# One result buffer for two attentions, table rows on GpSimd's queue, the last norm's weights inside w_up's pages, and ties for late rows

## The chip, the cores and the metric

One core of a Trainium2 chip runs the whole layer in one launch. The metric is the time of the program on the device in microseconds (us), lower is better. Before the change the median of 3 runs is 2635.41 us (2632.22 to 2638.98).

## What is computed

One layer of an encoder, in float32, for 2048 tokens of 1024 features:

```
h  = RMSNorm(x) * norm_mix
z  = h @ W_in          -> q_a k_a v_a q_b k_b v_b gate_a gate_b    (1024 x 4352)
yA = attention in a window of +-128 tokens, 8 heads on 2 kv heads, ALiBi slopes, a sink logit per head
yB = attention of 8 heads on a 32 x 64 grid, 8 x 16 neighbours, a learned bias table rpb per head
x  = x + (sigmoid(gate_a)*(yA @ Wp_A) + sigmoid(gate_b)*(yB @ Wp_B)) @ W_out
x  = x + relu(RMSNorm(x)*norm_mlp @ W_up)^2 @ W_down                (1024 x 4096, 4096 x 1024)
out = RMSNorm(x) * norm_final
```

## The kernel before

**Products.** Each float32 operand is split into a high and a low part (`split`, L281: a cast on ScalarE, L282, and a subtraction on VectorE, L283), and each product of tiles is three matmuls (hi*hi, hi*lo, lo*hi: `mm3s`, L286 to L288; for narrower tiles `mm3`, L202 to L204). The large products go in seven block products instead of eight (Strassen), so that VectorE also adds and subtracts blocks ahead of the split (L279) and adds results as they leave PSUM (L279 again, and L1560 where a gate is multiplied in). TensorE is fed without a break only if these casts, subtractions and loads are early enough.

**Order.** The program is written stage by stage with generators; a scheduler with a model of times decides the order in each engine's queue, `tc.issue_after(x)` keeps what is inside it behind instruction x, and buffers (pools, rings) decide what must wait for whom. Each engine works its queue in order. Nearly all transfers are issued by SyncE (SP), in order too: a transfer that waits for its buffer holds up every transfer behind it. ScalarE issues a few, and GpSimd some (L690, L721).

**Stages, with the times at which they run in the trace.**

- *Input*, to 554 us. x is loaded in tiles of 128 tokens, normalised and transposed. `rstd_of` (L220) makes the sum of squares of a tile in two ScalarE instructions (L225) with their accumulators, an addition on VectorE (L228) and a power on GpSimd (L230); `normalised` (L233) scales on VectorE (L239) for the first four tiles and on ScalarE (L237) for the others. z is then made in column groups q = 0 to 10 (`in_quad`, `in_seeded`), each of seven products. In `in_seeded` products 1, 5 and 6 leave PSUM by a ScalarE copy to another bank or buffer (the *seeds*, L532, L535), and the next products wait for these. Between the steps of a group stands preparation: in groups 3 and 4 the normalised rows of x (L784) and their transposition (`turned_out`), and from group 9 on W_out's operands (`wo_parts`, with L687 and L688). Results go out through a ring `ze` to tables in HBM.
- *Attention A*, 554 to about 820 us, 32 units of `attn_a` (L829): scores (L844, L845), max, exp, transposes to PSUM (L863), the casts of the probabilities `ph` on ScalarE (L867) and the remainders `pl` on VectorE (L868), then the products with v (L869, L870). Between these, TensorE does the gates' columns of z as filler (`gate_tiles`, L910 ff).
- *Attention B*, to about 1120 us: 32 units of `attn_b` (L1038), 4 per head: scores (L1056) of `qb` with `kb`, the bias added and the max taken (L1061), exp (L1067), scaling on GpSimd (L1072), transposes (L1084), casts `phb` (L1090) and remainders `plb` (L1091), the products with `vb` (L1096). `load_k` (L1029) loads one head's `kb` in three transfers (L1033 to L1035), L1046 loads `vb`. `make_bias_b` (L1009) loads rows of a table into `braw` (L1018, on SP), and GpSimd adds the masks (L1024). Filler is again `gate_tiles`, then `proj_tiles` (yA @ Wp_A), for which `y_pages` (L938) loads yA and splits it in eight casts (L948) and eight subtractions (L949).
- *Merge and W_out*, about 1120 to 1415 us, in two halves m of the tokens: `gated` (L1544) does yB @ Wp_B and the gates, `out_operands` (L1451) loads W_out's prepared parts from HBM into the ring `pgl` (`wo_d`, L1458; 6 places) and splits the left operands into the same ring, `out_products` (L1472) does the seven products, each in two halves of 24 matmuls, product 1's result copied between PSUM banks by L1498. In m = 1, rows of half 0 are normalised, transposed on VectorE (L249), multiplied by norm_mlp (`turned_gain`, L254) and written to HBM (`h2d`, L257).
- *w_up and w_down*, from about 1380 us to the end: `up_right` (L1299) makes the split pages of h2 for the seven products, `up_quad` (L1370) does them.

**PSUM and the change of attentions.** The four PSUM pools of the attentions are made in the order mm, s, pt, av (L800). SBUF's left side holds for A: dist, sta, qa, ka1, va1, sa, ya, ph, pl; after it, in the same addresses, for B: sb0, sb1, sb2, vb0, vb1, vb2, phb, plb, yb. So what of B lies on what of A decides how early B's loads may start. `ya` has two buffers of 64 partitions, `yb` one of B's own.

Of the kernel before, what the change touches and what calls it, by code (L numbers as in the profile page):

```python
# [92 lines left out]
def encoder_layer(ctx, tc, x, norm_mix, w_in, b_gate, sink, rpb, w_pa, w_pb, w_out,  # L93
# [126 lines left out]
    def rstd_of(pl, t, jp=None, mean=False, small=False):  # L220

        st = T(pl, [P, 4], F32, "st", 4)
        junk = T(pl if jp is None else jp, [P, 512], mybir.dt.bfloat16 if small else F32, "junk", 1)
        for n in range(2):
            A.activation(junk, t[:, n * 512 : (n + 1) * 512], AF.Square, scale=float(D) ** -0.5 if mean else 1.0,  # L225
                         accum_out=st[:, n : n + 1])
# [6 lines left out]
    def normalised(pl, tiles, jp=None, by_scalar=False, small=False):  # L233

        for t in tiles:
            if by_scalar:
                A.activation(t, t, AF.Copy, scale=rstd_of(pl, t, jp, True, small))  # L237
            else:
                V.tensor_scalar(t, t, rstd_of(pl, t, jp), float(D) ** 0.5, ALU.mult, ALU.mult)  # L239

    def turned_out(d, ht, tiles, g, gain=None):
# [9 lines left out]
        if gain is not None:  # L251
            (step, n), _ = gain.ap
            gv = bass.AP(gain.tensor, gain.offset + 8 * g, [[step, n], [1, 8], [0, P]])
            V.tensor_tensor(out=h3, in0=h3, in1=gv, op=ALU.mult)  # L254
# [4 lines left out]
    def turned_gain(t, norm):  # L259

        for a in range(4):
            SY.dma_start(t[32 * a : 32 * a + 32, 32:64], norm[0].rearrange("(j i) -> j i", i=32))
        V.transpose(out=t[:, 0:32], in_=t[:, 32:64])
        return t[:, 0:32]
# [247 lines left out]
    ORDER_3 = (1, 5, 6, 2, 7, 3, 4)  # L512

    def in_seeded(c, w, lf, right, b0=0):
# [3 lines left out]
        for n in ORDER_3:  # L518
            hl, (rh, rl) = next(lf), right[n]
            for a in range(w // P):  # L520
# [9 lines left out]
                if n == 1:  # L530
                    y[a] = zbank(ypool[a])
                    A.copy(y[a], ps)  # L532
                elif n == 5:
                    c22[a] = in_c()
                    A.copy(c22[a], ps)  # L535
                elif n == 6:
                    u2[a] = in_c()
                    A.copy(u2[a], ps)
# [15 lines left out]
    def scaled_less(out, ps, k, t):  # L554
        V.scalar_tensor_tensor(out=out, in0=ps, scalar=g_mix[:, k : k + 1], in1=t, op0=ALU.mult, op1=ALU.subtract)
# [24 lines left out]
    normalised(xp, tiles[0])  # L580
# [14 lines left out]
    normalised(xp, tiles[1], by_scalar=True)  # L595
# [112 lines left out]
    def h1_sums(k):  # L708
# [6 lines left out]
        yield  # L715
        for t, p in ((lo, 0), (hi, 1)):
            scaled(t, t, 4 * p + k)
# [38 lines left out]
    right2, n_wo = {}, [0]  # L756
    for q in range(2, len(QUADS)):
        prep, steps, b0 = iter(()), 1, 0
# [7 lines left out]
        elif q == len(QUADS) - 1:  # L766
            prep = h1_last(right2)
        elif q >= SECOND and QUADS[q][1] == 256:
            n_wo[0] += 1
            prep = wo_parts(n_wo[0], own)  # L770
# [20 lines left out]
        for _ in prep:  # L791
            pass
# [7 lines left out]
    pps.update({t: pool(f"pp_{t}", space=PSUM, stack=s_pp) for t in ("mm", "s", "pt", "av")})  # L800
    s_w = ExitStack()
    wp = pools(s_w, "right", ("raw", "whl", "z"), "w")
    s_a = ExitStack()
    ap_ = pools(s_a, "left", ("dist", "sta", "qa", "ka1", "va1", "sa", "ya", "ph", "pl"), "a")
# [12 lines left out]
    marks, began = [], []  # L817

# [10 lines left out]
    def attn_a(g, i):  # L829
# [41 lines left out]
        t = T(ap_, [64, 512], F32, "ya", 2)  # L871
        A.copy(t, po[64:128, :])
        V.tensor_tensor(out=t, in0=po[0:64, :], in1=t, op=ALU.add)
# [64 lines left out]
    def y_pages(b0):  # L938

        for b in (b0, b0 + 1):  # L940
            ypages[b] = [in_page[(6, 3, 1, 2)[b]]() for _ in range(2)]
            for g in range(2):
                SY.dma_start(halves(ypages[b][1])[g].bitcast(F32),
                             y_a[g][:, b * BT : (b + 1) * BT].rearrange("(c p) t -> p c t", p=P))
        with tc.issue_after(casts[min(now[0] + 4, len(casts) - 1)]):
            for b in (b0, b0 + 1):
                for h, l in zip(*map(halves, ypages[b])):
                    A.copy(h, l.bitcast(F32))  # L948
                    V.tensor_tensor(out=l, in0=l.bitcast(F32), in1=h.bitcast(F32), op=ALU.subtract)  # L949

# [34 lines left out]
    for n, g, m in ((4, 0, 0), (9, 0, 1), (14, 1, 1)):  # L985
        drive((attn_a(*u) for u in units_a[at:n]), live, False)
# [4 lines left out]
    drive((attn_a(g, i) for g, i in units_a[14:]), live, True)  # L991
# [11 lines left out]
    yb = T(bp, [P, BT], F32, "yb", 1)  # L1003
# [5 lines left out]
    def make_bias_b(h, jt):  # L1009
        j = (0, 1, 3)[jt]  # L1010
        w = B_W[j]
        t = T(bp, [P, 40 * w], F32, "biasl" if jt == 1 else "biass", 1 if jt == 1 else 2)
# [4 lines left out]
        with tc.issue_after(began[20]):  # L1017
            SY.dma_start(raw, src)  # L1018
# [89 lines left out]
    def all_b():  # L1108
        for h in range(BH):
            k = load_k(h)  # L1110

            for n, j in enumerate((0, 3, 1, 2) if h == 0 else range(4)):
                if j != 2:
                    bias = make_bias_b(h, JT[j])
# [20 lines left out]
    s_b.close()  # L1135
    s_pg = ExitStack()
# [36 lines left out]
    p4x = pools(s_wo, "left", ("junk", "gt", "ht", "xr"), "m")  # L1173
# [5 lines left out]
    gain = turned_gain(T(p4x, [P, P], F32, "gt", 1), norm_mlp)  # L1179
# [119 lines left out]
    def up_right(m):  # L1299
# [10 lines left out]
        def parts(n, src):  # L1310
            hi, lo = up_page[n](), up_page[n]()
            for s, h, l, e in zip(halves(src), halves(hi), halves(lo), (V, V)):
                last = split(s, h, l, e)
# [3 lines left out]
        def less(out, a, c):  # L1317
            for o, x, y in zip(halves(out), halves(a), halves(c)):
                add(V, o, x, y, ALU.subtract)
# [26 lines left out]
        less(t, b12, b11)  # L1346
        parts(1, b11)
        parts(5, t)
        yield
        b22 = block(up_rings["raw"](), 1, 1)  # L1350
        less(b12, b22, b12)
        less(t, b22, t)
# [3 lines left out]
        parts(2, b21)  # L1356
        yield right
        parts(7, b12)
        less(b21, b21, t)
        parts(4, b21)  # L1360
        parts(3, b22)
# [89 lines left out]
    def out_operands(ms):  # L1451


        def half(n, h):
# [3 lines left out]
            SY.dma_start(w.bitcast(F32), wo_d[n][h].rearrange("k p z c -> p k z c"))  # L1458
# [9 lines left out]
        for n in ORDER_O:  # L1468
            for h in range(2):
                yield half(n, h)  # L1470
# [65 lines left out]
    for m in range(2):  # L1536
# [268 lines left out]
```

## Time and profile before

| | |
|---|---|
| median of 3 runs | 2635.41 us (2632.22 to 2638.98) |
| the profiled execution | 2637.54 us |
| its span, first to last instruction | 2635.7 us |
| TensorE busy | 2555.2 us, 11936 matmuls |
| before TensorE's first matmul / after its last | 7.8 us / 8.3 us |
| VectorE, ScalarE, GpSimd busy | 1712.1, 1307.6, 342.0 us |
| DMA | 553.22 MB, 210 GB/s over the span |

The span is 1.8 us shorter than the execution's own time, and the execution is 2.1 us above the median. The table of TensorE's waits names, for each line, what released it, the sum, the count and the longest. A table of windows gives busy time by engine in a stretch, then the TensorE clock granted in it (1.00 is full, 0.50 half), the busy share of the 16 DMA engines and GB/s.

### The profile page before, as it was taken

To read this page: it belongs to the slowest core of one execution; us is meant where nothing else is said; L and a number is where in the kernel's file an instruction comes from. 1 tells how busy PE (TensorE), PEld (TensorE's weight loads), DVE (VectorE), ACT (ScalarE), POOL (GpSimd) and SP (SyncE) were. 2 spreads that over 40 slices of the span, in tenths; PEclk is the share of its full clock that TensorE was granted. 3 is DMA by queue.
4 is the path that set the end of the run, shared out by engine and by line. 5 is a ranking of instruction groups with operands and counts; after the bars stand their busy time and mean duration, and the time that the engine had idled before them with its cause. 6 is when DMAs were issued, how large, how long until landed. Compare 5 with 4: busy or idle time off the path is not lost.

```text
span 2635.7 us, 34520 instructions
## 1 busy us (share of the span) xinstructions
PE 2555.2 (97%) x11936; PEld 2123.7 (81%) x11936; DVE 1712.1 (65%) x2696; ACT 1307.6 (50%) x2345; POOL 342.0 (13%) x460
## 2 busy tenths in 40 slices
PE   7999999999998989999999999999999999999998
PEld 6878787877887878887777888888887888888887
DVE  7857576666764567665687677676656634554766
ACT  7365464557775666523246555654444322322444
POOL 1001001133344655200000000000000000000011
PEclk9999999999999999999999999999999999999999
DMA  5768777764347898787798655854427935445555
GB/s 184 225 180 276 253 229 239 244 203 137 92 144 192 233 261 242 233 300 269 253 335 255 238 204 199 277 206 148 149 103 285 318 99 182 147 147 169 184 193 166
DMA packets 348160, 553.22 MB, mean 210 GB/s; under 512 B 30904, under 2 KB 152888, under 8 KB 345808
## 3 DMA queue, kind: packets, MB, share of 16 engines
q1 hardware_dynamic: 333520, 515.35, 61.1%
q10 hardware_dynamic: 10944, 24.12, 2.5%
q0 software_dynamic: 3520, 11.54, 1.2%
q8 instruction: 94, 1.54, 0.3%
q14 instruction: 82, 0.67, 0.1%
HBM read 364.19 MB, written 186.71 MB: 209 GB/s over the span
## 4 chain that ended last, share of the span: by engine, by line
PE 43%; DVE 3%; DMA 2%; SPq 1%; ACT 1%; issue 0%; POOL 0%; POOLq 0%; DVEq 0%; ACTq 0%
PE b L287 14%; PE b L288 14%; PE b L286 14%; SPq L257 1%; DMA dw<-in_w_down_dram 0%; DMA uraw<-h2d 0%; DVE xr L279 0%; DVE uraw L279 0%; DMA at<-uc 0%; DMA x2d<-xr 0%; DVE ubh L283 0%; DVE pgl L283 0%; DMA uraw<-in_w_up_dram 0%; DMA x<-x2d 0%; DVE uc L279 0%
## 5 line engine op out<-in xcount | busy, mean ns | idle before, releaser
L287 PE MATMUL b<-dwh,dah 128*128 128x512 f32 x896 | 348.9, 389 | 0.4 <-DVE dwh L283 0.4
L288 PE MATMUL b<-dwh,dah 128*128 128x512 f32 x896 | 348.0, 389 | 0.0
L286 PE MATMUL b<-dwh,dah 128*128 128x512 f32 x896 | 338.5, 389 | 1.7 <-ACT dwh L282 1.7
L282 ACT CAST dah<-da 128x1024 fp32r<-128x1024 f32 (+1 forms) x128 | 120.6, 943 | 367.6 <-PE b L288 250.5
L286 PE MATMUL zb<-zh,zwhl 128*128 128x512 f32 x728 | 286.0, 394 | 10.2 <-ACT zb L532 5.1
L288 PE MATMUL zb<-zh,zwhl 128*128 128x512 f32 x728 | 284.1, 392 | 1.2 <-DVE zwhl L283 1.2
L287 PE MATMUL zb<-zh,zwhl 128*128 128x512 f32 x728 | 284.8, 391 | 0.0
L283 DVE TENSOR_TENSOR dah<-da,dah 128x1024 fp32r<-128x1024 f32 (+1 forms) x128 | 139.4, 1091 | 218.5 <-ACT dah L282 215.6
L286 PE MATMUL b<-ubh,uwhlb 128*128 128x512 f32 x592 | 231.5, 391 | 5.1 <-ACT uwhlb L282 3.5
L287 PE MATMUL b<-ubh,uwhlb 128*128 128x512 f32 x592 | 231.1, 390 | 0.1
L288 PE MATMUL b<-ubh,uwhlb 128*128 128x512 f32 x592 | 229.9, 391 | 0.0
L286 PEld LDWEIGHTS b<-dwh,dah 128*128 128x128 f32 x896 | 168.2, 188 | 36.9 <-ACT dwh L282 2.1
L287 PEld LDWEIGHTS b<-dwh,dah 128*128 128x128 f32 x896 | 168.2, 188 | 35.7 <-DVE dwh L283 0.8
L288 PEld LDWEIGHTS b<-dwh,dah 128*128 128x128 f32 x896 | 168.2, 188 | 34.8
L279 DVE TENSOR_TENSOR uc<-b,uc 128x512 f32<-128x512 f32 x160 | 109.4, 690 | 118.7 <-PE b L288 109.4
L286 PEld LDWEIGHTS zb<-zh,zwhl 128*128 128x128 f32 x728 | 137.1, 188 | 42.4 <-ACT zb L532 6.8
L202 PE MATMUL mm<-zh,whl 128*128 128x512 f32 x368 | 159.3, 433 | 2.1 <-DVE z L970 1.5
L288 PEld LDWEIGHTS zb<-zh,zwhl 128*128 128x128 f32 x728 | 137.0, 188 | 30.1 <-DVE zwhl L283 2.0
L287 PEld LDWEIGHTS zb<-zh,zwhl 128*128 128x128 f32 x728 | 137.2, 188 | 27.9
L204 PE MATMUL mm<-zh,whl 128*128 128x512 f32 x368 | 147.0, 399 | 0.0
L203 PE MATMUL mm<-zh,whl 128*128 128x512 f32 x368 | 146.5, 398 | 0.0
L286 PEld LDWEIGHTS b<-ubh,uwhlb 128*128 128x128 f32 x592 | 111.6, 189 | 29.6 <-ACT uwhlb L282 3.9
(254 smaller groups left out, 5692.1 us busy)
## 6 DMA issues: line engine op xcount, KB each, us to landing
at<-uc SPq DMA_DIRECT2D x224, 256.0 KB
da<-at SPq DMA_DIRECT2D x96, 512.0 KB
dw<-in_w_down_dram SPq DMA_DIRECT2D x160, 256.0 KB
uraw<-in_w_up_dram SPq DMA_DIRECT2D x32, 1024.0 KB
pgl<-wo_d SPq DMA_DIRECT2D x28, 1024.0 KB
zraw<-in_w_in_dram SPq DMA_DIRECT2D x24, 1024.0 KB
z<-zg SPq DMA_DIRECT2D x64, 256.0 KB
qs_a<-ze SPq DMA_DIRECT2D x32, 256.0 KB
```

Source lines behind the costliest of these rows:

```text
L202: PE.matmul(ps, lh, rh, start=first, stop=False)
L203: PE.matmul(ps, lh, rl, start=False, stop=False)
L204: PE.matmul(ps, ll, rh, start=False, stop=last)
L257: last_dma[0] = SY.dma_start(dv[a][:, 8 * g : 8 * g + 8], h3[32 * a : 32 * a + 32]).ins
L279: return eng.tensor_tensor(out=out, in0=a, in1=b, op=op).ins
L282: A.copy(hi, src)
L283: return eng.tensor_tensor(out=lo, in0=src, in1=hi.bitcast(F32), op=ALU.subtract).ins
L286: PE.matmul(ps, lh, rh, start=first, stop=False, skip_group_check=True)
L287: PE.matmul(ps, lh, rl, start=False, stop=False, skip_group_check=True)
L288: PE.matmul(ps, ll, rh, start=False, stop=last, skip_group_check=True)
```

## The change

It has nine parts.

1. `rstd_of` can do the second half of the squares on VectorE (a tensor_tensor_reduce), and does for x's first eight tiles.
2. In groups 3 and 4 the normalised rows stand in steps 1 and 2, tied behind the last seed copy, and the transposition two steps later; before, all was written ahead of the group's first step.
3. `wo_parts` of group 9 runs over groups 9 and 10 (every second step, the rest left for group 10). `h1_sums` does its two scalings two steps later and behind a seed.
4. PSUM's pools are made in the order mm, av, s, pt.
5. `yb` moves out of B's pools and lives from before A to after B; `ya` is one buffer of 128 partitions. A's results go by turns into the lower and upper half of `ya`, then of `yb`. With that the left side holds for A: dist, sta, qa, ka1, va1, ya, sa, ph, pl; for B: sb0, sb1, vb0, vb1, sb2, vb2, phb, plb.
6. 22 of the 24 loads of `braw` are issued by GpSimd, one table ahead of the additions.
7. Each cast and subtraction of `y_pages` is tied behind a cast of its own, spread over later units; before, all four of a pair stood behind one.
8. `out_operands` issues both weight loads of a product together, ahead of the first half's operand.
9. `turned_gain` is gone. norm_mlp is multiplied in when `up_right` makes its pages: ScalarE's scaled copy in place of a cast, VectorE's scalar_tensor_tensor in place of a subtraction, both in pieces of 128x512.

The core of it:

```diff
-            A.activation(junk, t[:, n * 512 : (n + 1) * 512], AF.Square, ...)
+            if n and other is not None:
+                V.tensor_tensor_reduce(out=other(), in0=half, in1=half, ..., accum_out=st[:, 1:2])
+                continue
...
-            normalised(xp, xt, Junk(), by_scalar=True)
...
-            for _ in range(steps):
+            for _ in range(steps if q != SECOND or n % 2 else 0):
                 next(prep, None)
-            if q in (3, 4) and n < 4:
-                turned_out(h1d[q - 3], in_e().rearrange("p k x -> p (k x)"), xt, n)
+            if q in (3, 4) and 1 <= n < 3:
+                with tc.issue_after(seeded[0]):
+                    normalised(xp, xt[2 * n - 2 : 2 * n], Junk(), by_scalar=True)
+            if q in (3, 4) and n >= 3:
+                turned_out(h1d[q - 3], in_e().rearrange("p k x -> p (k x)"), xt, n - 3)
...
-    pps.update({t: pool(f"pp_{t}", space=PSUM, stack=s_pp) for t in ("mm", "s", "pt", "av")})
+    pps.update({t: pool(f"pp_{t}", space=PSUM, stack=s_pp) for t in ("mm", "av", "s", "pt")})
...
-        t = T(ap_, [64, 512], F32, "ya", 2)
+        e = u % 2 * 64
+        t = (ya if u % 4 < 2 else yb)[e : e + 64]
...
-                    A.copy(h, l.bitcast(F32))
+                with tc.issue_after(casts[min(at + 3 + n + n // 2, len(casts) - 1)]):
+                    A.copy(h, l.bitcast(F32))
                     V.tensor_tensor(out=l, in0=l.bitcast(F32), in1=h.bitcast(F32), op=ALU.subtract)
...
-    bp.update(pools(s_b, "left", ("sb0", "sb1", "sb2", "vb0", "vb1", "vb2", "phb", "plb", "yb"), "b"))
+    bp.update(pools(s_b, "left", ("sb0", "sb1", "vb0", "vb1", "sb2", "vb2", "phb", "plb"), "b"))
...
+        if n_raw[0] < 3:
+            with tc.issue_after(began[20]):
+                SY.dma_start(raw, src)
+        else:
+            G.dma_start(raw, src)
...
-            w = ring_l[0]()
-            SY.dma_start(w.bitcast(F32), wo_d[n][h].rearrange("k p z c -> p k z c"))
...
+            ws = [weights(n, h) for h in range(2)]
             for h in range(2):
-                yield half(n, h)
+                yield half(n, h, ws[h])
...
-                turned_out(h2d[i], T(p4x, [P, 2 * BT], F32, "ht", 1), old[i], f % 4, gain)
+                turned_out(h2d[i], T(p4x, [P, 2 * BT], F32, "ht", 1), old[i], f % 4)
...
+                for k in range(4):
+                    scaled(hi[:, k], src[:, k], 4 * p + k)
+                    last = scaled_less(lo[:, k], src[:, k], 4 * p + k, hi[:, k].bitcast(F32))
```

SP's queue where A ends and B begins; `vb` and `kb` belong to B's first units and to its heads 0 and 1, `zg` and `raw` to the filler. Before:

```order
L175 DMA y_a_143<-ya_7038 64x4x128
L1046 DMA vb_838_7507<-vs_b_92 96x4x256
L1018 DMA braw_845_7541<-tab_153 128x1x512
L1046 DMA vb_847_7548<-vs_b_92 96x4x256
L1046 DMA vb_854_7583<-vs_b_92 128x4x256
L175 DMA zg_105<-z_7402 128x512
L175 DMA y_a_143<-ya_7065 64x4x128
L189 DMA raw_8889<-in_w_in_dram 128x8x128
L1033 DMA kb_868_7669<-ks_b_88 128x2048
L1034 DMA kb_868_7669<-ks_b_88 64x2048
L1035 DMA kb_868_7669<-ks_b_88 64x2048
```

And of the change, the same stretch; the first `vb` stands eight rows above this piece:

```order
L175 DMA y_a_143<-yb_4489 64x4x128
L1047 DMA kb_846_7648<-ks_b_88 128x2048
L1048 DMA kb_846_7648<-ks_b_88 64x2048
L1060 DMA vb_832_7562<-vs_b_92 128x4x256
L1049 DMA kb_846_7648<-ks_b_88 64x2048
L175 DMA zg_105<-z_7383 128x512
L175 DMA y_a_143<-yb_4489 64x4x128
L189 DMA raw_8868<-in_w_in_dram 128x8x128
```

The second head's `kb` moved from behind A's last result and a filler load to ahead of both, and no `braw` stands between.

ScalarE's queue at the first pair of pages of `y_pages`; `phb` are casts that TensorE's next products wait for. Before:

```order
L1090 CAST phb_8755<-pt_8751 96x384
L1103 COPY yb_7484<-av_8655 64x512
L1090 CAST phb_8768<-pt_8763 96x512
L948 CAST zh_1083_9066<-zh_1084_9067 128x1024 x2
L948 CAST zh_1085_9070<-zh_1086_9071 128x1024 x2
L1090 CAST phb_8781<-pt_8776 96x512
L178 CAST whl_9009<-raw_9006 128x1024
```

And of the change:

```order
L1104 CAST phb_8734<-pt_8730 96x384
L954 CAST zh_1061_9045<-zh_1062_9046 128x1024
L1117 COPY yb_4489<-av_8634 64x512
L1104 CAST phb_8747<-pt_8742 96x512
L954 CAST zh_1061_9045<-zh_1062_9046 128x1024
L1104 CAST phb_8760<-pt_8755 96x512
L178 CAST whl_8988<-raw_8985 128x1024
L463 ACTIVATE z_9016<-mm_9061,bg 128x512
L1104 CAST phb_8772<-pt_8768 96x384
L954 CAST zh_1063_9053<-zh_1064_9054 128x1024 x2
```

Four casts in a row became one, one and two, with casts of `phb` between.

SP's queue at W_out's second product (m = 0); `wo_d_965` and `wo_d_973` are its weights in the two kernels, `wo_d_968` the third product's, `z` and `xr` loads for the gates and for x. Before; the product's first load stands 28 rows above the second, which is here:

```order
L1551 DMA z_12611<-zg_103 128x512
L1551 DMA z_12611<-zg_105 128x512
L1553 DMA z_12612<-zp_123 128x512
L1553 DMA z_12612<-zp_131 128x512
L1551 DMA z_12662<-zg_103 128x512
L1458 DMA pgl_11999<-wo_d_965 128x2x1024
L1551 DMA z_12662<-zg_105 128x512
L1458 DMA pgl_12068<-wo_d_968 128x2x1024
```

And of the change:

```order
L1487 DMA pgl_11962<-wo_d_973 128x2x1024
L1487 DMA pgl_11964<-wo_d_973 128x2x1024
L189 DMA raw_12725<-in_w_proj_b_dram 128x4x128 x2
L1588 DMA z_11889<-zp_112 128x512
L1588 DMA z_11889<-zp_120 128x512
L217 DMA xr_11923<-in_x_dram 128x1024
```

The product's second load moved up past 27 rows to stand behind its first.

More of the change, by code (lines that the diff above doesn't have):

```diff
@@ L594, in encoder_layer @@
     next(quad0)
-    normalised(xp, tiles[1], by_scalar=True)
+    normalised(xp, tiles[1], by_scalar=True, other=in_c)
     next(quad1)
@@ L938, in y_pages @@
     def y_pages(b0):
+        at, n = now[0], 0
         for b in (b0, b0 + 1):
@@ L942, in y_pages @@
             for g in range(2):
[L943 to L947, printed above, removed]
+                h, l = (halves(t)[g] for t in ypages[b])
+                SY.dma_start(l.bitcast(F32), y_a[g][:, b * BT : (b + 1) * BT].rearrange("(c p) t -> p c t", p=P))
+                with tc.issue_after(casts[min(at + 3 + n + n // 2, len(casts) - 1)]):
                     A.copy(h, l.bitcast(F32))
                     V.tensor_tensor(out=l, in0=l.bitcast(F32), in1=h.bitcast(F32), op=ALU.subtract)
+                n += 1
     casts, now = [], [0]
@@ L1016, in make_bias_b @@
         src = bass.AP(tabs[jt].tensor, tabs[jt].offset + first, [[w, 8], [1, 16], [1, 16 * w]])
-        with tc.issue_after(began[20]):
-            SY.dma_start(raw, src)
+        if n_raw[0] < 3:
[3 more added lines that the diff above has]
+            G.dma_start(raw, src)
+        return raw
+    def make_bias_b(raw, jt):
+        j = (0, 1, 3)[jt]
+        w = B_W[j]
+        t = T(bp, [P, 40 * w], F32, "biasl" if jt == 1 else "biass", 1 if jt == 1 else 2)
         for i in (0, 1, 3):
@@ L1108, in all_b @@
     def all_b():
+        order = [(h, j) for h in range(BH) for j in ((0, 3, 1, 2) if h == 0 else range(4))]
+        tables = [(h, JT[j]) for h, j in order if j != 2]
+        raws = [load_raw(*tables.pop(0))]
         for h in range(BH):
@@ L1345, in up_right @@
         t = up_rings["raw"]()
-        less(t, b12, b11)
-        parts(1, b11)
-        parts(5, t)
+        for o, x, y in zip(*map(halves, (t, b12, b11))):
+            add(V, o, x, y, ALU.subtract)
+        parts(1, b11, 0)
+        parts(5, t, 0)
         yield
+        gained(t, 0)
+        gained(b12, 0)
         b22 = block(up_rings["raw"](), 1, 1)
-        less(b12, b22, b12)
-        less(t, b22, t)
+        gained_less(t, b22, 1, t)
         parts(6, t)
```

114 lines of the change are left out of this document (64 added, 50 removed).

## The prediction

> **What bounds the kernel now.** I read the page's busy times first, then windows by stage, then the table of TensorE's waits, and last the clock granted behind the long waits.
>
> From the page, busy time and count by engine:
>
> ```profile
> PE 2555.2 (97%) x11936; PEld 2123.7 (81%) x11936; DVE 1712.1 (65%) x2696; ACT 1307.6 (50%) x2345; POOL 342.0 (13%) x460
> ```
>
> Windows by stage: input, the two attentions, merge with W_out, then w_up and w_down. The number behind each comma and name is busy time in us; behind POOL stand the clock, the DMA share, GB/s.
>
> ```profile
> 12.00:554.00 542.00, 522.90 (x2338) 427.61 (x2338) 369.56 (x460) 288.43 (x425) 48.42 (x73) 1.00 0.73 229
> 554.00:1130.00 576.00, 552.27 (x3113) 476.43 (x3114) 373.96 (x969) 371.24 (x954) 267.24 (x342) 0.98 0.68 188
> 1130.00:1436.00 306.00, 288.27 (x1234) 233.94 (x1233) 218.14 (x296) 112.82 (x166) 8.79 (x16) 0.98 0.85 291
> 1436.00:2635.70 1199.70, 1187.77 (x5237) 982.69 (x5235) 747.30 (x966) 527.28 (x782) 14.61 (x17) 1.00 0.55 190
> ```
>
> TensorE bounds every stage. The change keeps all 11936 matmuls, so only its idle time can go: 19 us in the input, 24 in the attentions, 18 in the merge, 12 in the last 1200 us, which the change does not touch. The waits by name (sum, times, longest):
>
> ```profile
> PE zb L276 <- DVE xin L239: 8.3, 2, 7.8
> PE av L1096 <- DVE plb L1091: 7.1, 6, 3.4
> PE b L286 <- DMA pgl<-wo_d: 5.6, 2, 4.9
> PE s L1056 <- DMA kb<-ks_b: 5.4, 3, 4.3
> PE zb L286 <- ACT zb L532: 5.1, 3, 2.5
> PE b L286 <- ACT uwhlb L282: 3.5, 1, 3.5
> PE s L844 <- DVE ze L428: 3.0, 1, 3.0
> PE b L202 <- DVE z L1560: 2.4, 1, 2.4
> PE b L286 <- ACT b L1498: 2.1, 1, 2.1
> ...
> PE zb L276 <- ACT xin L237: 1.6, 1, 1.6
> ...
> PE av L1096 <- DMA vb<-vs_b: 1.6, 1, 1.6
> PE zb L286 <- DVE zc L279: 1.6, 2, 1.3
> ```
>
> A long wait costs twice. These windows begin where each of seven long waits ends; the last begins behind a wait of 1.6 us:
>
> ```profile
> 411.00:414.50 3.50, 3.50 (x10) 2.74 (x11) 1.67 (x2) 0.73 (x2) 0.00 (x0) 0.59 0.95 251
> 555.00:562.00 7.00, 7.00 (x22) 5.65 (x22) 1.48 (x7) 2.11 (x9) 0.00 (x0) 0.60 0.65 172
> 837.80:844.60 6.80, 6.80 (x27) 6.22 (x28) 1.60 (x7) 1.01 (x2) 2.83 (x3) 0.55 1.14 330
> 944.20:950.00 5.80, 5.79 (x21) 5.22 (x22) 2.65 (x7) 2.42 (x8) 5.80 (x7) 0.52 0.97 226
> 977.30:981.00 3.70, 3.67 (x13) 3.29 (x14) 2.22 (x6) 1.26 (x4) 0.83 (x1) 0.57 0.39 114
> 1204.80:1211.00 6.20, 6.20 (x18) 4.93 (x19) 4.31 (x5) 0.72 (x2) 0.00 (x0) 0.65 0.67 269
> 1429.70:1434.00 4.30, 4.30 (x13) 3.44 (x14) 4.30 (x6) 0.00 (x0) 0.00 (x0) 0.66 1.05 386
> 1727.00:1731.00 4.00, 4.00 (x18) 3.31 (x19) 3.97 (x6) 1.35 (x3) 0.00 (x0) 1.00 0.90 304
> ```
>
> Window times (1 - clock) is the time lost: 1.4, 2.8, 3.1, 2.8, 1.6, 2.2 and 1.5 us, 15.4 in all; after the short wait nothing. So a wait of 2 us or more costs its length and 1.4 to 3.1 us.
>
> The Trainium skill ("TensorE: Matmul & The Clock Gate", What's actually happening) says that the clock halves after an idle window of about 3.4 us. The rows differ: the waits of 2.5 and 3.0 us were followed by 0.59 and 0.60. By the page neither the wait at 411 nor the one at 944 would cost clock, and the sum below would gain 2.9 us less (1.4 x 0.85 + 2.8 x 0.61, the shares counted there); the rows decide.
>
> **The change part by part**, against the profiled execution of 2637.5 us. Negative is faster; bounds in brackets.
>
> *Squares on VectorE.* For the first four tiles VectorE's own chain (normalise, add, and the wait for GpSimd's power) already has the pace of the tiles' arrival, so TensorE's first matmul at 7.8 us stays: 0 (-0.7 to +0.5). For the next four, ScalarE loses four squares ahead of its L237, for which TensorE waits 1.6 us: -1.3 (-1.6 to 0, if L555's pages come later behind the new VectorE work).
>
> *Rows in groups 3 and 4.* Two of the three waits for L532 (5.1 less the 2.5 at 411 = 2.6 us), and the 1.3 us for L279 on zc, arise while ScalarE works through squares ahead of the seeds. The seeds now come first: -2.5 of 3.9 (-3.9 to 0, if the squares only make the next seeds late).
>
> *wo_parts over two groups.* The wait at 411 follows this: ScalarE waits for a buffer of `ze`, whose store is late, and the seed is queued behind.
>
> ```profile
> 408.32 0.60 ACT L431 ACTIVATE ze<-zb 128x512 fp32r<-128x512 f32 x1 [1.39 <-DMA qs_a<-ze]
> ```
>
> With half the preparation gone from group 9, VectorE and ScalarE reach `ze` earlier, and its stores too. I take 2.5 + 1.4 by 0.85: -3.3 (-3.9 to 0, as the store's own time stays).
>
> *PSUM's order at 555.* Three scores may start before the last input result has left. The fourth needs VectorE's max (L846), which stands behind that same L428 in VectorE's queue. I read that the 3.0 us wait moves to the fourth score: 0 (-5.8 to +1). The value at hand is 0, since the last L428 stays where it was.
>
> *Attention A to B.* In order of SP's queue:
>
> ```profile
> 811.46 0.59 SPq L175 DMA_DIRECT2D y_a<-ya  x1
> ...
> 827.40 0.33 SPq L1033 DMA_DIRECT2D kb<-ks_b  x1
> ```
>
> The first row is the last result but one of A, the second the first of the three transfers of head 1's `kb`. Between them stood the first `vb`, waiting for `va1`, which A's last product reads, and a filler load. Now `vb` lies on `ka1`, free at A's last scores, and `kb` stands right behind that result: some 16 us earlier, four times the 4.3 us for which TensorE waited. The three costs are 4.3 + 3.1 + 1.6 (vb) = 9.0. Head 0's `kb` now shares the DMA engines with an early `vb`, which can cost 1 or 2 us: -7 (-9 to -3).
>
> *Table rows on GpSimd.* The trace has no `braw` from GpSimd. The nearest rows are GpSimd's own transfers of 256 KB, and what GpSimd now waits for `braw`:
>
> ```profile
> L690 POOL DMA_DIRECT2D wo_d<-xin x28: 539/539/768, 219.5 to 509.4; - x28
> ```
>
> ```profile
>   POOL biass L1024: 11.4, 4
>   POOL biasl L1024: 9.1, 2
> ```
>
> 22 issues at 0.54 to 0.77 us are 12 to 17 us of an engine that is busy 267 of 576 us here and waits 20.5 us for these rows now; behind each issue stand L1024 and L1072, for which TensorE's transposes (L1084) wait last. Hidden by that idle time: 0; the price without cover is a rival below.
>
> *y_pages.* ScalarE does four casts in one piece, and casts of `phb` queue behind; VectorE's subtractions follow in pairs:
>
> ```profile
> 936.74 3.90 ACT L948 CAST zh<-zh 128x1024 fp32r<-128x1024 f32 x4
> ```
>
> ```profile
> 941.20 2.35 DVE L949 TENSOR_TENSOR zh<-zh,zh 128x1024 fp32r<-128x1024 f32 x2
> ```
>
> Around them lie nearly all of the 7.1 us of waits for `plb`, and 2.8 + 1.6 us of clock: 11.5. One at a time, a cast delays `phb` by 1.0 and `plb` by 1.2 us, below what halves the clock; but one pair stays together, and some of the waits come back small: -7 (-11.5 to -2).
>
> *W_out's weights in pairs.* The wait is 4.9 us, with 2.2 of clock. The load behind it was issued here, while the DMA engines were full:
>
> ```profile
> 1197.46 0.37 SPq L1458 DMA_DIRECT2D pgl<-wo_d  x1
> ```
>
> ```profile
> 1160.00:1208.50 48.50, 43.59 (x185) 35.64 (x184) 35.81 (x39) 14.99 (x21) 0.00 (x0) 0.94 1.05 385
> ```
>
> It moves up to its product's first load, 27 rows ahead, so this wait goes. But 1 MB at 385 GB/s is 2.7 us by which everything between comes later, up to the third product's weights, needed one half after the fourth half begins. By the last stage's row a matmul takes 1187.77 / 5237 = 0.227 us, a half of 24 thus 5.4. The left operands lose one such half of lead, of which a cast and a subtraction (the yA rows, 1.0 and 1.2 each) take 2.2. -5.5 (-7.1 to 0).
>
> *norm_mlp into the pages.* Removed and added work:
>
> ```profile
> L254 DVE TENSOR_TENSOR ht<-ht,gt x8: 1204/1218/1227, 1257.1 to 1348.9; 128x1024 f32<-128x1024 f32 x8
> ```
>
> ```profile
> L555 DVE SCALAR_TENSOR_TENSOR zh<-xin,g_mix,zh x16: 739/746/2519, 332.7 to 530.3; 128x512 fp32r<-128x512 f32 x16
> ```
>
> Eight L254 are 9.7 us of VectorE ahead of 1350. In `up_right` 28 pieces of 0.75 replace 14 instructions of L254's size at 1.22 us: 21.0 - 17.1 = +3.9 later, and some 6 us more on ScalarE. In m = 1 the gates (L1560, 2.4 us) profit; the wait for L1498 (2.1) stays, since the copy stands behind casts that wait for h2 from HBM: -2 (-4.5 to +3, if w_up's loads crowd out `pgl`). At w_up's start the 3.5 us (L282) with 1.5 of clock come from VectorE's backlog, which is 9.7 - 3.9 = 5.8 us shorter, while ScalarE's is longer: -2.5 (-5.0 to +0.5).
>
> *New places.* In 576 us of attention the scheduler interleaves anew. The waits under 2 us there that I named nowhere sum to about 24 - 3.0 - 4.3 - 1.6 - 7.1 = 8 us; I add half as many again: +4 (0 to +12).
>
> Sum: 0 - 1.3 - 2.5 - 3.3 + 0 - 7 + 0 - 7 - 5.5 - 2 - 2.5 + 4 = -27.1 us, so 2610.4 in the profiled execution. That one lies 2.1 above the median, hence **2608.3**, 1.0% faster.
>
> **The rivals.** *Bytes only shift.* The DMA engines are full in 1160 to 1208.5, and `kb` lands late again or the W_out wait moves to the next product. Then the W_out term is 0, A to B is half, and m = 1 costs 3 instead of giving 2: -27.1 + 5.5 + 3.5 + 5 = -13, so 2622. For it speaks the share of 1.05; against it that the bytes before each deadline hardly grow.
>
> *Waits only move*, so that the ties do not do what they say: seeds, `ze` and `phb` cannot come earlier since the engines ahead of them are as full as before. Then groups 3 and 4, the wait at 411 and y_pages give nothing: -27.1 + 2.5 + 3.3 + 7 = -14, 2621. For it speaks that the wait at 555 moves in just this way; against it ScalarE's 371 busy of 576 us.
>
> *Slower: GpSimd becomes the bound of B.* Its mechanism: an issue of 128 rows takes long, and the four scalings behind it keep TensorE from its transposes. GpSimd has about 576 - 267 = 309 us idle over all, near 14 us for each issue, but in order only what lies between a unit's max and its transposes counts, one or two fillers of 6 matmuls, some 3 us. From 3.5 us an issue it decides; at 5 us each of 22 tables would cost 2 us and some 2 us of clock, 22 x 4 = 88, and if half of them meet cover still 44: 2608 + 44 = 2652. Against it stands 0.54 to 0.77 us in 28 rows.
>
> The Trainium skill ("SBUF — State Buffer", A bandwidth-pool intuition that's wrong) states that a transfer issued by GpSimd can stall from about 620 to 3100 ns while VectorE holds the port they share. By that figure as an estimate the 22 issues would take 68 us in place of 12, still within GpSimd's idle time; no run here shows such an issue yet.
>
> **How the numbers follow.** Forecast (within about 9 us of 2608) 0.58; bytes shift 0.14; waits only move 0.12; GpSimd bounds 0.05; better than forecast, the favourable ends of A to B, y_pages and 555 together (-9 -11.5 -5.8 in place of -14, 2596 and below) 0.11. The two middle rivals at once give 0 to -5 us and are counted in their shares. The favourable ends of all terms would sum to -53, the unfavourable to +12; neither end is likely, since they hardly meet. Range 2592 to 2634: below it 0.07, above it 0.12. A change of 0.3% (7.9 us) is about what a measurement tells from none: faster 0.82, same 0.11 (the rivals joined, 2627 to 2643), slower 0.07.
>
> **What would show it.** Right: no wait of `kb` over 1 us and no half clock near 838; no four casts of yA in a row and no wait over 2 us for `plb`; W_out's third half without a wait; seeds ahead of squares in groups 3 and 4. At 555 a wait of about 3 us should stand at a later score (L844). Wrong: new waits of 2 us or more inside B with clock 0.5 behind them, GpSimd's issues over 3 us, waits for `pgl` at 1205 or 1340, or a later first matmul than 7.8 us.

## The result, and the profile after

The changed kernel's median is 2622.45 us (2618.99 to 2623.36, 5 runs), beside 2636.84 us for the kernel before on the same chip: a ratio of 0.9944 (95% interval 0.9930 to 0.9959). Run once more on another occasion it gave 0.9956 (0.9941 to 0.9971). That is 12 to 15 us of 2636; the forecast was 27. In the profiles the span fell from 2635.7 to 2620.7 us.

TensorE's waits in the changed kernel, as name, sum, count and longest:

```profile
PE zb L269 <- DVE xin L243: 8.1, 3, 7.3
PE b L279 <- DMA pgl<-wo_d: 5.0, 3, 4.2
PE av L1110 <- DVE plb L1105: 4.8, 10, 1.0
PE b L279 <- ACT uwhlb L275: 4.5, 1, 4.5
PE av L1110 <- DMA vb<-vs_b: 4.3, 2, 3.7
PE b L279 <- ACT pgl L275: 3.4, 1, 3.4
PE s L1070 <- DMA kb<-ks_b: 3.1, 2, 2.2
PE s L1070 <- DMA qb<-qs_b: 3.0, 1, 3.0
```

The seeds' long waits (L532) are gone, and so are the 1.6 us for L237 and the 2.4 us for the gates. The waits for `plb` are now ten short ones. One of 3.4 us, for a cast of W_out's left operand (`pgl`), is new. W_out's weights (4.2 us) and w_up's operand (4.5) are waited for nearly as long as before or longer, `kb` half as long, and two others have grown: `vb` to 3.7 us in the middle of B, and `qb` to 3.0 at its start.

The table sets the forecast beside the profiles, by stretches between matmuls (first score of A, last product of B, last product of W_out). "Seeds alone" is the kernel before with two parts of the change, described below; the profiled execution of it lies 6.2 us above its median.

| stretch, us | before | changed | changed again | seeds alone | forecast | changed - before |
|---|---|---|---|---|---|---|
| start to first score of A | 550.9 | 538.9 | 539.6 | 540.4 | -7.1 | -12.0 |
| to B's last product | 572.4 | 574.0 | 573.2 | 572.4 | -10.0 | +1.6 |
| to W_out's last product | 273.0 | 266.7 | 267.6 | 275.3 | -7.5 | -6.3 |
| to the end of TensorE's work | 1230.8 | 1232.7 | 1230.9 | 1231.2 | -2.5 | +1.9 |

The two attentions gave nothing of the 10 us, though the long waits for `plb` and the first one for `vb` did go and that for `kb` was halved. The input gave 12.0 where 7.1 was forecast. The rest asks why.

### The profile page after: what moved, and what is told of

Its sections match the earlier page's. It is cut to its first block, busy times and chain, and to the rows that moved or that the text cites. A ratio compares the mean times of both kernels' runs of the same rounds, so it can differ in the third digit from the quotient of the medians.

```text
span 2620.7 us, 34535 instructions
## 1 busy us (share of the span) xinstructions
PE 2551.7 (97%) x11936; PEld 2123.5 (81%) x11936; DVE 1710.1 (65%) x2717; ACT 1309.0 (50%) x2345; POOL 354.3 (14%) x482
## 4 chain that ended last, share of the span: by engine, by line
PE 75%; DMA 13%; DVE 6%; ACT 3%; SPq 2%; issue 2%; POOL 0%; DVEq 0%; POOLq 0%; ACTq 0%
PE b L280 15%; PE b L279 15%; PE b L281 15%; PE zb L281 5%; PE zb L279 5%; PE zb L280 5%; PE mm L202 2%; PE mm L204 2%; PE mm L203 2%; DMA vb<-vs_b 2%; DMA h2d<-ht 1%; PE av L1110 1%; PE pt L869 1%; DMA z<-zg 1%; PE pt L1098 1%
```

## The experiments

The theory, from the two traces: at the change of attentions, in parts of B, and at W_out the 16 DMA engines set the time. An earlier issue then mostly makes a transfer wait longer, and TensorE gives back what it won. Windows of the changed kernel, with clock, DMA share and GB/s at the end, for B's beginning and two pieces of B:

```profile
808.00:836.00 28.00, 22.79 (x122) 20.08 (x121) 14.43 (x42) 13.97 (x38) 14.95 (x19) 0.88 1.08 235
836.00:990.00 154.00, 147.71 (x910) 130.50 (x909) 100.62 (x246) 105.07 (x255) 103.80 (x122) 1.00 0.96 241
990.00:1035.00 45.00, 39.12 (x237) 33.92 (x235) 27.30 (x68) 23.15 (x61) 24.34 (x32) 0.98 0.89 241
```

The rivals: GpSimd's transfers push SP's back; SP's queue stands still for other reasons; or the forecast's terms are right and another part costs 12 us. Where nothing else is said, an experiment is the changed kernel with one edit.

**Rows of the tables on SP's queue again.**

```diff
-            G.dma_start(raw, src)
+            SY.dma_start(raw, src)
```

> The changed kernel with all 24 loads of table rows issued by SyncE again, everything else as changed. Theory (at the change of attentions the DMA engines are full, share 1.05 from 808 to 836 us, and the loads of kb and qb wait for bytes, whoever issues them): the waits for kb (2.2 us at 823) and qb (3.0 us at 829) stay within 1.5 us in sum, as does the 3.7 us for vb at 1034; time within 3 us of the changed kernel. Rival (GpSimd's own transfers push SyncE's back): these waits, 8.9 us with 5.7 us of half clock, shrink to under 3 us and the time falls by 5 to 10 us. Second rival (GpSimd's queue is what freed SyncE's): SyncE stands still for rows again, kb is issued later and the time rises by 5 us or more.

Measured: 0.9959 (0.9946 to 0.9971), span 2622.0. The wait for `kb` comes at 788 (3.2 us), the wait for `qb` goes, and `vb` at 1035 is waited for 5.0 us: 8.2 us for the three where it was 8.9. From A's first score to B's last product it takes 574.9 us. Head 1's `kb` is issued 6 us later here (809.5 for 803.4), without a longer wait for it. The waits change places and the sum stays: neither rival holds.

**The old result buffers and order of the left side.**

```diff
-    ("sb0", "sb1", "vb0", "vb1", "sb2", "vb2", "phb", "plb")
+    ("sb0", "sb1", "sb2", "vb0", "vb1", "vb2", "phb", "plb", "yb")
...
+        t = T(ap_, [64, 512], F32, "ya", 2)
```

> The changed kernel with the result buffers and the order of the left side as before (vb0 on va1 again, two buffers of ya, yb among B's). My forecast put 9 us on this part together with the rows' queue. If the forecast's mechanism holds, the wait for kb at 823 grows to over 4 us and vb waits 1.5 us again: 5 to 9 us slower than the changed kernel. Theory (full DMA engines take back what the earlier issue gives): within 3 us of the changed kernel, with the same sum of waits, some 5 to 7 us between 780 and 850.

Measured: 0.9958 (0.9942 to 0.9975), span 2623.3. The first wait for `vb` is back, at 811 and longer than before (3.9 us), and that for `kb` is only 1.4 us; from A's first score to B's last product 575.7 us, against 573 to 574. By these single profiles the part is worth about 2 us, and the ratios don't part it from 0; nothing shows the forecast's 7.

**Half of k's loads left out in heads 2 to 7.**

```diff
+        if h < 2:
+            kbs.append(T(bp, [P, 2, S], F32R, f"kb{h % 2}", 1))
+        k = kbs[h % 2]
         SY.dma_start(k[:, 0].bitcast(F32), kd)
+        if h >= 2:
+            return k
```

> The changed kernel with heads 2 to 7 of attention B loading one of their two copies of k (1 MB in place of 2 MB; the other copy stays that of heads 0 and 1, so this leaves out part of the work). Theory (transfers bound B's waits for vb): the waits for vb at 993 and 1034 (0.6 and 3.7 us, 3.3 us of half clock behind the second) go, B is 5 to 8 us shorter; the waits for kb and qb near 823 to 829, of heads 0 and 1, stay; the 4.2 us at 1197 stays or grows, as W_out is reached earlier. Rival (vb waits in SyncE's queue behind other waits): vb's wait stays over 2 us.

Measured: 0.9904 (0.9889 to 0.9919), span 2610.3. The same two pieces of B in its windows:

```profile
836.00:990.00 154.00, 150.59 (x936) 134.14 (x935) 104.31 (x255) 107.46 (x262) 106.65 (x126) 1.00 0.81 229
990.00:1035.00 45.00, 44.43 (x280) 40.05 (x279) 31.64 (x80) 27.55 (x71) 27.10 (x34) 1.00 0.78 235
```

TensorE gains 26 and 43 matmuls in these pieces, no wait for `vb` is left, and the way from A's first score to B's last product is 562.5 us, 11 us shorter. Taking 6 MB away did what no reordering did, so in B the transfers cost TensorE this time. The edit also takes 12 issues out of SP's queue, but the changed kernel's own rows speak against the queue as the cause. The `vb` that TensorE waited for at 1034 had been issued 15 us before, and by the trace it landed at 1034.2:

```profile
1019.11 0.58 SPq L1060 DMA_DIRECT2D vb<-vs_b  x1
```

```profile
1034.36 0.55 PE L1110 MATMUL av<-phb,vb 96*128 96x256 f32 x1 [3.74 <-DMA vb<-vs_b]
```

The wait of 4.1 us for W_out's weights stayed.

**W_out's weights apart again.**

```diff
-            ws = [weights(n, h) for h in range(2)]
-                yield half(n, h, ws[h])
+                yield half(n, h, weights(n, h))
```

> The changed kernel with W_out's two weight loads of a product issued one by one again, as before. Theory (bytes bound this stage, the pairing only moves the wait from the fourth half to the third product): a wait of 4 to 5 us for pgl one half earlier, time within 2 us of the changed kernel. Forecast's own mechanism: slower by 5 us or more.

Measured: 0.9966 (0.9952 to 0.9979), span 2621.2. The wait for `pgl` is 7.6 us, at the fourth half, with another of 3.4 us in m = 1:

```profile
PE b L279 <- DMA pgl<-wo_d: 11.5, 3, 7.6
```

From B's last product to W_out's it took 270.1 us against 266.7 and 267.6. That would make the pairing worth some 3 us, but the stretch varies as much without it: the run with PSUM's old order, below, keeps the pairs and took 270.8. The ratio doesn't part it from the changed kernel's either. What the trace does show is that without the pairing the wait is longer than it was before the change (7.6 for 4.9).

**Fewer bytes ahead of the third product's weights.**

```diff
-            if n < 2:
-                rows[1].extend(x_row(m, 1, 2 * n + t) for t in range(2))
+            if m == 0 and n == 1:
+                with tc.issue_after(w_last[0]):
+                    rows[1].extend(x_row(m, 1, t) for t in range(4))
```

> The changed kernel with the four loads of x's rows for the second quarter of W_out's first half (2 MB) tied behind the third product's weights. Theory (bytes ahead of those weights bound them): 2 MB at 361 to 393 GB/s are 5 us, so the weights land 4 to 5 us earlier, the wait of 4.2 us at 1197 falls below 1 us with its 1.6 us of half clock; 4 to 6 us faster, if the rows still come ahead of product 5's results. Rival (the weights wait in SyncE's queue for z's buffers, not for bytes): they are issued within 1 us of 1190 as now and the wait stays 3 us or more; time within 2 us.

Measured: 0.9930 (0.9915 to 0.9946), 2614.23 us, span 2609.6. In SP's queue of this kernel the weights and behind them the rows:

```profile
1181.20 1.00 SPq L1489 DMA_DIRECT2D pgl<-wo_d  x2
1182.51 2.30 SPq L217 DMA_DIRECT2D xr<-in_x_dram  x4
```

W_out begins at 1166.6 here, so the issue is 14.6 us later; in the changed kernel 18.8 (from 1171.1 to 1189.86, by a row shown further below). The wait is gone with its half clock, and from W_out's first product to the gates' last one takes 119.7 us for 125.4, hence 5.7 us. The rest of the profile's 11 us lies mostly in B, which the edit doesn't touch, and is one execution's chance; this one was 2.9 us below the median. SP's issue itself came 4.2 us earlier, which neither theory said, and which is as much as the wait itself. Some 3 us of it are the issues that moved (five rows of x took 3.64 us of SP's queue, one is left with 0.33), and 1.5 the loads of `yraw` (4.44 us for four, now 2.94). So the late rows pay, but this run does not tell the bytes from SP's queue.

**norm_mlp multiplied in by VectorE again** (the code of before for `turned_gain`, `turned_out` and `up_right`).

> The changed kernel with norm_mlp multiplied in by VectorE in the second half's rows again (eight more instructions of 1.2 us there) and w_up's pages split as before. Theory (the pages' scaled copies put 6 us more on ScalarE, which is what TensorE now waits for at 1322, 3.4 us, and at 1414, 4.5 us): both waits fall by about 1 us each with some of the half clock behind them, the wait of 2.4 us for the gates (L1595) near 1290 comes back; within 2 us of the changed kernel. The forecast's mechanism (VectorE's shorter backlog gives 4.5 us): slower by 3 to 6 us. Rival (these waits are for transfers of h2 and have nothing to do with the gain): both waits stay within 0.5 us of 3.4 and 4.5, the gates' wait comes back: slower by 1 to 3 us.

Measured: 0.9938 (0.9919 to 0.9957), span 2616.6. The long waits at w_up's start are gone but for one of 1.1 us, and W_out's last product to the end takes 1227.8 us, 3 to 5 us less; the gates' wait did not come back, and from B's last product to W_out's it takes 267.1 us, as in the changed kernel. So moving the gain is not what took the gates' wait away. No theory said this, and the last run below, with the same edit, has a wait there again.

**PSUM's pools in the old order.**

```diff
-    ("mm", "av", "s", "pt")
+    ("mm", "s", "pt", "av")
```

> The changed kernel with PSUM's pools in the order before (mm, s, pt, av). My forecast had it at 0, a wait that moves; the trace of the changed kernel has fillers between the third and the fourth score, which hide it. Theory: the first score waits for the last input result again, 2 to 3 us with 2 to 3 us of half clock, less the 1.9 us that the first score waits for qa now; slower by 3 to 4 us. Rival (the store of the last results, not PSUM, bounds the start): within 1 us.

Measured: 0.9937 (0.9914 to 0.9961), span 2623.2. The wait is back, as TensorE's row shows:

```profile
542.78 0.39 PE L850 MATMUL s<-ka,qa 128*128 128x256 f32 x1 [2.42 <-DVE ze L421]
```

But the wait of 1.9 us for `qa` at A's first score is gone in its place, and B's first score comes at 781.3 us in both kernels, so the part's net there is 0.

**yA's pages in bursts of four casts again.**

```diff
+        with tc.issue_after(casts[min(now[0] + 4, len(casts) - 1)]):
+            for b in (b0, b0 + 1):
+                for h, l in zip(*map(halves, ypages[b])):
```

> The changed kernel with the eight casts of yA's pages behind two ties again, four in a row. Theory (the burst on ScalarE and VectorE makes phb and plb late): waits of 2 to 3.4 us for plb near 930 and 965, half clock behind both, slower by 5 to 8 us. Rival (the transfers bound this stretch, so casts that are late cost what transfers would have cost): within 2 us, with fewer waits for DMA behind it.

Measured: 0.9963 (0.9951 to 0.9976), span 2619.8. Its waits in B:

```profile
PE av L1110 <- DVE plb L1105: 5.6, 7, 2.9
PE s L1070 <- DMA kb<-ks_b: 5.2, 3, 2.2
...
PE av L1110 <- ACT phb L1104: 4.1, 2, 3.6
...
PE av L1110 <- DMA vb<-vs_b: 2.3, 1, 2.3
```

The waits of 2.9 and 3.6 us come back with their half clock, and the wait for `vb` is shorter. B takes 308.9 us from its first product with v, against 309.5 and 306.0 in the two profiles of the changed kernel. By the traces the part is worth 0 to 3 us. But the profiled execution took 2621.54 us, 5.5 below the median of 2627.09, so its trace may not show what the others lost. The ratios (0.9963 against 0.9944 and 0.9956) say 2 to 5, with intervals that overlap, and on this run's own chip the two kernels above, whose edits change little, had medians of 2619.94 and 2620.92: 6 to 7 us less. So what the part is worth stays open between 0 and the forecast's 7.

**The input stage's two parts undone** (rows of groups 3 and 4 ahead of the seeds, W_out's preparation all in group 9). The edit also puts back the two scalings of `h1_sums` in the next groups, which belong to the change's third part.

> The changed kernel with the rows of groups 3 and 4 normalised ahead of the groups' first step, and W_out's preparation crowded into group 9, as before. Theory (seeds late behind squares and behind stores of ze): waits of 1.2 to 1.3 us at about 174, 178 and 201 and 2.5 us at 410 come back with 1.4 us of half clock, 6.6 to 9 us slower at the end of the input stage; and 3 us of it are won back where the transfers bound W_out: 4 to 6 us slower over all. Rival (nothing is won back behind): slower over all by as much as the input stage, 6.6 to 9 us.

Measured: 0.9995 (0.9983 to 1.0008), 2633.61 us. The whole gain is gone, more than the theory or the rival said. The seeds are waited for again, the copies' followers (`zc`) for longer than before, and also the transposes' sources (`ze`), which I had not put on this account:

```profile
PE zb L279 <- ACT zb L526: 4.6, 3, 2.4
...
PE zb L390 <- DVE ze L404: 3.0, 2, 2.4
...
PE zb L279 <- DVE zc L272: 2.7, 2, 1.6
```

**These two parts alone,** on the kernel before, with the scalings of `h1_sums` again among them.

> The kernel before with only the change's two parts on the input stage: rows of groups 3 and 4 behind the seeds, W_out's preparation spread over two groups. Theory (nearly all of the change's gain is these two, since undoing them costs 11 to 13 us): the first score 8 to 12 us earlier than before, the whole 8 to 12 us faster, 0.9955 to 0.997. Rival (they help only with the other parts beside them, and the transfers behind take part of it back): 3 to 6 us faster, with longer waits for kb and for W_out's weights than before (over 4.3 and over 4.9 us).

Measured: 0.9959 (0.9944 to 0.9973), 2623.15 us, where the whole change gave 2621.5 on the same chip. The first score comes at 540.4, 10.5 us earlier. The waits of the kernel before are nearly all there behind it, and W_out's has grown, in an execution of 2629.33 us, 6.2 above the median:

```profile
PE b L286 <- DMA pgl<-wo_d: 8.1, 3, 7.3
...
PE av L1105 <- DVE plb L1100: 7.9, 6, 3.4
PE s L1065 <- DMA kb<-ks_b: 7.2, 3, 5.5
```

So the rival was right about the longer waits (7.3 for 4.9, 5.5 for 4.3), and the theory about the size. B's last product comes at 1112.8 us here and at 1112.8 in the changed kernel's second profile: by these two profiles, what the other parts do inside the attentions is worth nothing in sum. By the medians all other parts together are worth 1.7 us, which the intervals don't part from 0.

What each tie in the input gave can be read by setting each of the 2328 matmuls into `zb` beside the same one in the kernel before. The changed kernel is 1.2 us behind at 120 us, 3.5 ahead at 220, 6.2 at 300 and 10.5 at 420; with the two parts alone it is 1.9 behind, then 2.9, 5.8 and 10.1 ahead. So the rows of groups 3 and 4 gave 4.7 and 4.8 us, what lies between 220 and 300 gave 2.7 and 2.9, and W_out's preparation 4.3. The middle step falls where the scalings of `h1_sums` run. In the kernel before ScalarE stood still there until a load for one of them had landed. The cast and the subtraction for `ze` were queued behind it on ScalarE and VectorE, and TensorE waited 1.4 us for `ze`:

```profile
275.07 1.15 ACT L552 ACTIVATE xin<-xin,g_mix 128x1024 f32<-128x1024 f32 x1 [4.79 <-DMA xin<-h1d]
```

```profile
277.60 0.33 PE L397 MATMUL zb<-ident,zc 128*128 128x128 f32 x1 [1.40 <-DVE ze L411]
```

The runs undo this tie only together with the rows', so its share is read from the traces and not tested alone.

**The changed kernel again**, beside these.

> The changed kernel once more, unaltered, to stand on the same chip beside the three others. Expected: 0.9944 of the time before within its interval (0.993 to 0.996), the profile's waits as in its first profile within 1.5 us each where a transfer is waited for.

Measured: 0.9956, span 2619.7. Two waits differ by more than 1.5 us (`vb` has 2.7 and 2.2 where it had 0.6 and 3.7; the wait for w_up's operand at 1415 is 1.6 for 4.5, with one of 2.2 for `ubh`): where the DMA engines are full, the single wait is chance to 2 or 3 us. From A's first score to B's last product the two profiles differ by 0.8 us, and the one with the late rows, whose edit lies behind, by 3 to 4.

**Rows late and VectorE's gain together.**

> The changed kernel with two edits at once: x's rows of the second quarter behind the third product's weights, and norm_mlp multiplied in by VectorE again. Each took away its own wait (4.2 us with 1.6 us of clock at 1197; 4.5 us with 2.2 us of clock at 1414). Theory (they are apart, so they add): spans of -11 and -4 us in the single profiles, of which about 4 us of the first lay in B and may be chance: 8 to 13 us faster than the changed kernel, ratio 0.989 to 0.9915. Rival (the later start takes it back): within 3 us of the better single one, 0.9925 to 0.9935.

Measured: 0.9918 (0.9905 to 0.9931), 2613.08 us, span 2612.3: 8.4 us below the changed kernel's 2621.5 on the same chip, faster than the kernel before and the changed one, though not clearly faster than the late rows alone. The rows' part holds (120.5 us from W_out's first product to the gates' last). The other's doesn't: W_out's last product to the end is 1232.0 us again, with this wait:

```profile
PE b L290 <- ACT ubh L286: 4.4, 1, 4.4
```

## Why the prediction came out as it did

The direction held, and the time lies in the range; the size was half of the forecast, by terms that erred in both directions. That they left the time in the range is in part luck.

*Squares.* The first matmul is at 7.3 for 7.8 us, the wait for L237 fell from 1.65 to 0.43, as forecast. In time the -1.3 is not shown: at 100 us the changed kernel's matmuls come 0.4 to 0.5 us later than the same ones before, though 1 us earlier than with the two parts alone.

*Rows and preparation in the input:* forecast -5.8, measured -10.5 alone and -10 to -13 when undone. The mechanism was right. The rows' term was too small by half (-2.5 for 4.7 measured), W_out's preparation by a quarter (-3.3 for 4.3), and the tie of `h1_sums` had no term at all, where the traces show 2.7 to 2.9. Alone, 2 us of it are given back at W_out (275.3 for 273.0); in the whole change none.

*PSUM's order:* the step "the fourth needs VectorE's max" failed as to what stands between. The trace has 14 filler matmuls between the third and the fourth score, and the wait left there is this one:

```profile
543.53 0.39 PE L850 MATMUL s<-ka,qa 128*128 128x256 f32 x1 [0.50 <-DVE sta L852]
```

The 3.0 us did move, to the load of `qa` at the first score (1.9 us). The net of 0 came out, by another way than forecast, as the run with the old order shows.

*Attention A to B:* the step that failed is "some 16 us earlier, four times the 4.3 us for which TensorE waited". By the rows of SP's queue `kb` was issued 12 us earlier counted from A's first score. But TensorE's score came only 2.9 us earlier by that count, because 17.9 us now lie between the issue of `kb`'s third transfer and the end of TensorE's wait. Before the change it was 8.4 (829.28 to 837.70). In the changed kernel, the first and the third transfer and the score that waits:

```profile
803.36 0.33 SPq L1047 DMA_DIRECT2D kb<-ks_b  x1
```

```profile
804.91 1.08 SPq L1049 DMA_DIRECT2D kb<-ks_b  x1
```

```profile
822.77 0.55 PE L1070 MATMUL s<-kb,qb 128*128 128x288 f32 x2 [2.19 <-DMA kb<-ks_b]
```

The lead was real; the DMA engines, at a share of 1.08 in that stretch, took most of it back. -7 became 0 to -2.

*y_pages:* the burst and its long waits did go, as forecast. What that is worth stays open between 0 and -7, as its run says. In the changed kernel's profiles waits for `vb` stand in B in their place, and there the transfers bound the time, as the run with half of k's loads shows. Whether the +4 for new places was of the right size can't be told while this term is open; the waits that came are for transfers, and not for a new interleaving.

*W_out's weights:* -5.5 for a part worth perhaps 3. The wait didn't go, it moved one half on, to the third product's weights, as the rival had it, here in SP's queue of the changed kernel:

```profile
1189.86 4.06 SPq L1487 DMA_DIRECT2D pgl<-wo_d  x4
```

The step that failed: I had set 2.7 us of delay for what lies between against a half of 5.4 us for the third product's weights, and counted the gain. They were issued 18.8 us after W_out's start and came 4.2 us late. In m = 1 the waits for the gates (2.4) and for L1498 (2.1) went, and the one of 3.4 for the left operand's cast came; the whole stretch gave -6.3 of -7.5. Which part gave that isn't shown.

*norm_mlp:* at w_up's start -2.5 was forecast and 0 to +2 measured. Undoing it took that start's waits away once and not the second time. Whether ScalarE's longer pages or the transfers of h2 decide there stays open: in one run the wait is for the weights' cast, in another for that of h2.

*GpSimd's issues:* the rival didn't come.

```profile
L1026 POOL DMA_DIRECT2D braw<-tab x22: 600/646/676, 739.8 to 1020.7; - x22
```

They took 0.65 us each, within the bounds of 0.54 to 0.77. The Trainium skill ("SBUF — State Buffer", A bandwidth-pool intuition that's wrong) has about 3100 ns for a transfer that GpSimd issues beside a copy on VectorE. None of the 22 issues took that long, but no plain copy ran on VectorE beside them, so the page's case isn't tested here.

The rival of the shifted bytes, to which I gave 0.14, names what happened in the attentions and the wait that moved at W_out. 2622 was its time too, but by luck: it had -6.5 for the attentions, which measured +1.6, and +3 for the stretch to W_out's last product, which measured -6.3, and the input gave 5 us more.

## What to carry to other kernels

Before a wait for a transfer is counted as a gain, read the DMA share of the stretch. Where it was 0.9 and more here, 12 us of earlier issue brought TensorE's work 2.9 us forward, while taking 6 MB of transfers away shortened B by 11. So add up what must land by the deadline, at the rate of that stretch: a nearly full share was 241 GB/s in B and 385 at W_out. In the input, with a share of 0.73, taking away the instruction that stands ahead of a producer paid in full, and more than the waits that named it. A group of parts undone in the changed kernel, and the same group alone on the kernel before, tell together whether it carries the change; look in each of the two diffs for what else the edit moves.

## What the runs showed of the hardware

A transfer's issue on SP, usually 0.3 to 0.6 us, took 4.8 us while the share was above 1, and held up the queue behind it; in the changed kernel a result of B was delayed so, and `qb` behind it:

```profile
817.60 4.80 SPq L175 DMA_DIRECT2D y_b<-yb  x1
```

Waits near 2 us are sometimes followed by half the clock and sometimes not. In the changed kernel, 1.9 at 539 was not, and 2.2 at 823 with 3.0 at 829 was, for 6.8 us. In the kernel before, the 2.4 us for the gates at 1302 were not, so the prediction's "2 us or more" is no firm bound; and in the changed kernel's second profile waits of 1.7, 0.9 and 0.2 us between 952 and 957 were followed by 3.4 us of it. The same rows of `braw` moved mostly in packets of 4096 and 4608 bytes from GpSimd's queue and of 1536 and 2048 from SP's, with no difference in the kernel's time that could be measured.
